# Dense expert products ahead of the lists, dense buffers in three pools, a third set of split halves, gelu two steps later, planner rate 430

## The chip, the core and the metric

The kernel runs on one core of a Trainium2 chip. The core has a matrix engine (TensorE, in the profile PE, its weight loads PEld), a vector engine (DVE), an activation engine (ACT), GpSimd (POOL), which issues the gathers here, and SyncE (SP), which issues the plain loads. The metric is the device time of one launch in microseconds, as the median over runs.

## What is computed

One residual layer over 1024 tokens of width 1024: three token mixers on a normalised input, gated and summed, and then an expert mixer (PEER). Only the second half matters here, cut to its core:

```python
q = (hf @ w_q).reshape(T, 8, 2, 128)
sc = jnp.einsum('thpd,hpkd->thpk', q, subkeys)
s1, i1 = lax.top_k(sc[:, :, 0], 16)
s2, i2 = lax.top_k(sc[:, :, 1], 16)
cand = (s1[..., :, None] + s2[..., None, :]).reshape(T, 8, 256)
top_s, pos = lax.top_k(cand, 16)
idx = jnp.take_along_axis(cand_idx, pos, axis=-1)   # of 16384 experts
gate = jax.nn.softmax(top_s, axis=-1)
act = jax.nn.gelu(jnp.einsum('chkd,cd->chk', u[ic], hc), approximate=False)
out = jnp.einsum('chk,chkd->cd', gate * act, v[ic])
```

Each token picks 16 of 16384 experts in each of 8 heads; each picked expert is a row of `u` and a row of `v`, of 4 KB each.

## The kernel before

**Tokens.** The 1024 tokens are 8 tiles of 128. The front (mixers, projections, norm, expert queries) runs in three groups of 2, 3 and 3 tiles (`GROUPS`, function `phase1`). After a group, `topk` (line 963) makes the lists of experts of its tiles in small steps that are kept in `side` and handed out one at a time by `sides` (line 1369).

**Two ways to the experts.** Six tiles gather: class `Experts` fetches by indirect DMA from POOL one row of `u` for each of 128 tokens (`fetch`, line 1082), DVE multiplies and sums it with the token (`step`, line 1122), a gelu of 32 such results follows on ACT, and 34 steps after the row of `u` the row of `v` is fetched; PE adds four rows of `v` at a time into two banks (`sum`, line 1155). That is 768 fetches of `u` and 768 of `v`. There are 5 buffers for rows of `u`, 8 for rows of `v`.

The tiles 4 and 6 (`DENSE`) are computed densely, over all 16384 experts: 128 blocks `e` of 128 experts, 256 tokens. For a block: a product with `u` and a gelu; a multiplication with the gate matrix; a product with `v` summed over all blocks in four banks. Two forms of the product with `u` exist. `early` takes plain f32 operands, for the first `RUN` = 22 blocks, and its results wait in `w`. `product` takes operands split into a high and a low half (`split`: ACT copies the high half, DVE subtracts to get the low one), three matmuls for each piece of the depth. The products with `v` (`weigh` and the loop behind it) use split halves of `v` and of `w`.

**Order in `dense` (line 1234).** It waits until the lists of both dense tiles are stored (`while len(stored) < ND`), with 1500 ns booked for each empty step. Then `wait[0]` stops the lists, the tokens are loaded, and `gate_matrix` (line 1192) builds the gate matrix for the last of the two tiles in 80 steps; every fifth step runs one `early`. The rest of the 22 follow, then the main loop: in step `e` the product of block `e + 22`, `weigh(e + 1)`, and the four banks' sums of block `e`. `take` makes the halves of `u` one block ahead; `weigh` makes those of `v` in the step before their use.

**Buffers.** `front.close()` gives back the front's memory (pools `const`, `wp`, `wide`, `big`, `act`, `kvp`, `tmp`, `small`, in this order of addresses); the dense part's one pool `dp` is laid over all of it. Scores from which the lists are made lie in `sc`, which is not part of the front, and for the middle tile of a group of three in `wide`, which is.

**The planner.** What is interleaved with what is fixed when the program is built. The loop at the end of `block_kernel` keeps two clocks in ns, `pe` and `dma`. A step of the gather (one row of `u`, one of `v`) adds 520 ns for the sum to `pe` and its bytes over `bw` to `dma`; a step of the front or of `dense` (`fill`) adds the estimate of its matmuls times `slow` and its loads over `bw`. `due` moves on at least 1500 ns for each kind of row in a step.

```python
least = LEAST * ((len(ex.todo) > 0) + (len(ex.vs) > 0))
due = max(due + least, pe - least)
while filler[0] is not None and (dma > pe or pe < due):
    a, b = fill(1)
```

`fill(1)` also hands out one step of the lists. `BW` is the rate in bytes per ns in the front (305) and after it (460). ACT and POOL run in program order; the order on the other engines is set by the scheduler of the language.

Of the kernel before, what the change touches and what calls it, by code (L numbers as in the profile page):

```python
# [7 lines left out]
F32 = mybir.dt.float32  # L8
# [26 lines left out]
RUN = 22  # L35


BW = 305.0, 460.0
SLOW = 1.38, 1.1
SUM_NS, ROW_BYTES = 520.0, 128 * 4096 + 12 * 1024.0  # L40
LEAST = 1500.0
# [38 lines left out]
def block_kernel(ctx: ExitStack, tc: tile.TileContext, io):  # L80
# [29 lines left out]
    def bank():  # L110
        return ps.tile([128, 512], F32, name="bank")
# [963 lines left out]
    class Experts:  # L1075
# [46 lines left out]
        def step(self):  # L1122

            self.run_behind()
            if not self.todo:
                return
            t, k = self.todo.pop(0)
            u = self.us.pop(0)
            nc.vector.scalar_tensor_tensor(u, u, 1.0, t["h"], op0=OP.mult, op1=OP.mult,  # L1129
                                           accum_out=t["parts"][:, k:k + 1])  # L1130
            b, c, j = k // 32, k % 32 // QB, k % QB
            self.behind.append([None] * (VLAG - 1) + [lambda: self.fetch("v", t["iT"][:, c, j, b:b + 1])]
                               + [None] * (SLAG - VLAG - 1) + [(lambda: self.sum(t, b, c, j)) if j % SUMS == SUMS - 1 else None])
            if k % 32 == 31:
                self.behind.append([lambda: self.gelu(t, b), lambda: self.scale(t, b), None,
                                    lambda: self.turn(t), lambda: self.weights(t, 0)])

        def gelu(self, t, b):
# [94 lines left out]

    def dense():
        st = ctx.enter_context(ExitStack())
        dp = st.enter_context(tc.tile_pool(name="dp", bufs=2))
        late_pool.append(dp)
        while len(stored) < ND:
            cost[0] += 1500
            yield  # L1240
        wait[0] = True
        whole = dp.tile([128, C, D], F32, name="vr")
        for i in range(ND):
            load(whole[:, i].rearrange("p (k t) -> p k t", k=KD), h2d[i])
        hh = dp.tile([128, KD, TD], F32R, name="hh", bufs=1)
        hl = dp.tile([128, KD, TD], F32R, name="hl", bufs=1)

        def split_tokens():
            for i in range(ND):
                r = whole[:, i].rearrange("p (k t) -> p k t", k=KD)  # L1250
                c = slice(i * 128, (i + 1) * 128)
                actf(hh[:, :, c], r, AF.Copy)
                nc.vector.tensor_sub(hl[:, :, c], r, hh[:, :, c])

        def raw(src, name):
            r = dp.tile([128, C, D], F32, name=name)
            load(r, src)
            return r

        def split(r, x, name):  # L1260
            hi = dp.tile([128, D], F32R, name=name + "h")
            lo = dp.tile([128, D], F32R, name=name + "l")
            actf(hi, r[:, x], AF.Copy)
            nc.vector.tensor_sub(lo, r[:, x], hi)  # L1264
            return hi, lo

        ur, us, ws, vr, gts = {}, {}, {}, {}, {}

        def near(e):
            if e % C == 0:  # L1270
# [1 line left out]
            return ur[e // C]  # L1272

        def take(e):
            us[e] = split(near(e), e % C, "u")

        def early(e):
            a = bank()[:, :TD].rearrange("p (i t) -> p i t", i=ND)
# [5 lines left out]
            actf(w.rearrange("p (i t) -> p i t", i=ND), a, AF.Gelu)  # L1284

        def product(e, a):
            if e + 1 < 128:
                take(e + 1)
            uh, ul = us.pop(e)
            for k in range(KD):  # L1290
                kc = slice(k * 128, (k + 1) * 128)
                mmr(a, uh[:, kc], hh[:, k, :], start=k == 0, stop=False, skip_group_check=True)
                mmr(a, ul[:, kc], hh[:, k, :], start=False, stop=False, skip_group_check=True)
                mmr(a, uh[:, kc], hl[:, k, :], start=False, stop=k == KD - 1, skip_group_check=True)
            w = ws[e] = dp.tile([128, TD], F32, name="w", bufs=RUN + 2)
            actf(w, a, AF.Gelu)
# [3 lines left out]
                gts[b] = dp.tile([128, TD // 32, 8, 32], F32, name="g")  # L1300
                load(gts[b], gd[:, :, 8 * b:8 * b + 8, :].rearrange("b p i t -> p b i t"))

        ur[0] = raw(io["uT"][0], "ur")
        e = steps = 0
        while next(gates) < ND:
            steps += 1
            cost[0] += 800
# [1 line left out]
                early(e)  # L1309
                e += 1  # L1310
            yield
        split_tokens()
        early(e)
        gate_load(0)
        vr[0] = raw(io["vd"][0], "vr")
        for e in range(e + 1, RUN):
            yield
            early(e)
        take(RUN)
        yield  # L1320
        behind[0], wait[0] = True, False

        sums = [[bank() for _ in range(2)] for _ in range(ND)]
        ab = bank().rearrange("p (x n) -> p x n", x=2)

        def weigh(e):
            if e % 8 == 0:
# [1 line left out]
            w = ws.pop(e)  # L1329
            nc.vector.tensor_mul(w.rearrange("p (b t) -> p b t", t=32), w.rearrange("p (b t) -> p b t", t=32),  # L1330
                                 gts[e // 8][:, :, e % 8, :])
            wh = dp.tile([128, TD], F32R, name="wh")
            wl = dp.tile([128, TD], F32R, name="wl")
            actf(wh, w, AF.Copy)
            nc.vector.tensor_sub(wl, w, wh)
            if e % C == 0:
                vr[e // C + 1] = raw(io["vd"][e // C + 1], "vr") if e + C < 128 else None
            return wh, wl, *split(vr[e // C], e % C, "v")

        now = weigh(0)  # L1340
        for e in range(128):
            if e + RUN < 128:
# [12 lines left out]
                yield  # L1355
            now = nxt
        for i in range(ND):
            r = dp.tile([128, C, D], F32, name="ur")[:, 0]
            load(r, xres[DENSE[i]])
            for half in range(2):  # L1360
                f = slice(half * 512, (half + 1) * 512)
# [123 lines left out]
```

## Time and profile before

| what | value |
|---|---|
| time, three runs | 3655.71, 3656.19, 3662.34 us; median 3656.19 |
| the profiled execution | 3664.29 us, its span 3662.5 us, mean granted clock 0.935 |
| moved by DMA | 1182.29 MB, mean 323 GB/s over the span |
| rows of u on DVE (768) | 933.3 us busy, mean 1220 ns; 605.8 us idle before them, 508.9 of it for the row to land |
| products with split u (3 x 848 matmuls) | 244.3 + 243.0 + 242.0 us |
| products with split v (3 x 512 matmuls) | 212.5 + 212.2 + 208.3 us |

Page, part 2: the span in 40 slices of 91.6 us; each digit of the first rows is a share in tenths, PEclk the clock granted to PE.

```profile
PE   7999979988999889899889898946867888889899
DVE  5443597555444568886655554889756766666645
PEclk9999989998999999999999999968888999999999
DMA  4435678989899997899887999879999999999995
GB/s 160 123 117 169 209 250 327 370 308 342 307 384 366 391 348 278 309 343 374 299 317 279 364 360 377 300 277 393 389 387 398 410 409 402 379 385 392 382 358 180
```

The front ends in slice 27 (2405 us), where PE falls to 4 and 6 tenths; the dense main loop starts at about 2716 us, in slice 30. A busy PE is not PE at its peak: ends of matmuls are modelled and they overlap.

### The profile page before, as it was taken

The page shows a single profiled execution, that of the slowest core. Times are in us where ns is not written, and L with a number is a line of the kernel's source. Part 1 is how long each engine was busy: PE and PEld are TensorE (multiplying, and loading weights), DVE is VectorE, ACT ScalarE, POOL GpSimd, SP SyncE. Part 2 cuts the span into 40 slices and gives each one's busy share as a digit, 9 for nine tenths or more (in the row PEclk, how much of TensorE's full clock was granted, in tenths as well). Part 3 has the DMA queues.
Part 4 walks back from the last instruction along what each step waited for, and adds up shares of the span by engine and source line. Part 5 has one row for each costly group of instructions (what it writes and reads, how often), then busy time and mean ns, then how long its engine had stood idle before and what let it go on. Part 6 is the DMA issues. An engine that isn't in the chain of part 4 may idle for free.

```text
span 3662.5 us, 59007 instructions
## 1 busy us (share of the span) xinstructions
PE 3182.7 (87%) x22418; PEld 2381.9 (65%) x22418; DVE 2295.9 (63%) x5873; ACT 994.8 (27%) x2065; POOL 1764.4 (48%) x1543
## 2 busy tenths in 40 slices
PE   7999979988999889899889898946867888889899
PEld 6889856655556666666555557734655767777677
DVE  5443597555444568886655554889756766666645
ACT  4442223332100123342322111111222333333334
POOL 0000046645565555566454555356656665655540
PEclk9999989998999999999999999968888999999999
DMA  4435678989899997899887999879999999999995
GB/s 160 123 117 169 209 250 327 370 308 342 307 384 366 391 348 278 309 343 374 299 317 279 364 360 377 300 277 393 389 387 398 410 409 402 379 385 392 382 358 180
DMA packets 343084, 1182.29 MB, mean 323 GB/s; under 512 B 38480, under 2 KB 79952, under 8 KB 323344
## 3 DMA queue, kind: packets, MB, share of 16 engines
q0 software_dynamic: 221184, 805.40, 58.2%
q1 hardware_dynamic: 100848, 336.37, 25.2%
q10 hardware_dynamic: 20768, 36.74, 2.6%
q8 instruction: 177, 2.90, 0.3%
q14 instruction: 107, 0.88, 0.1%
HBM read 1140.61 MB, written 37.75 MB: 322 GB/s over the span
## 4 chain that ended last, share of the span: by engine, by line
PE 46%; DMA 17%; DVE 13%; issue 13%; POOL 5%; ACT 2%; another core or an unknown queue 2%; ACTq 0%; SPq 0%; POOLq 0%; DVEq 0%
PE bank L118 31%; PE bank L1184 8%; DMA u<-in_u,iI 7%; DMA v<-in_v,iT 6%; DVE u L1129 3%; POOL v L1085 3%; PE poa L1163 3%; PE pob L1163 3%; POOL u L1085 2%; PE bank L122 1%; DMA ur<-in_uT 1%; DMA w<-in_w_gate 1%; ACT e L129 1%; DVE ab L1208 1%
## 5 line engine op out<-in xcount | busy, mean ns | idle before, releaser
L1085 POOL DMA_INDIRECT u<-in_u,iI x768 | 881.0, 1147 | 950.8 <-DVE wide L330 471.9
L1129 DVE SCALAR_TENSOR_TENSOR u<-u,h 128x1024 f32<-128x1024 f32 x768 | 933.3, 1220 | 605.8 <-DMA u<-in_u,iI 508.9
L1085 POOL DMA_INDIRECT v<-in_v,iT x768 | 882.7, 1149 | 853.1 <-PE pob L1163 349.5
L118 PE MATMUL bank<-wide,w 128*128 128x384 f32 x1536 | 523.3, 495 | 14.2 <-DVE wide L330 5.3
L118 PEld LDWEIGHTS bank<-wide,w 128*128 128x128 f32 x1536 | 292.3, 193 | 219.1 <-issue 21.3
L118 PE MATMUL bank<-w,wide 128*128 128x128 f32 x2304 | 277.2, 279 | 20.4 <-issue 17.5
L118 PEld LDWEIGHTS bank<-w,wide 128*128 128x128 f32 x2304 | 267.7, 194 | 35.4 <-issue 28.0
L1163 PE MATMUL pob<-v,wz 128*32 128x256 f32 x3072 | 231.8, 414 | 66.7 <-DMA v<-in_v,iT 61.0
L1184 PE MATMUL bank<-hh,uh 128*128 128x256 f32 x848 | 244.3, 288 | 30.4 <-ACT uh L129 19.0
L1184 PE MATMUL bank<-vl,wh 128*128 128x512 f32 x512 | 212.5, 415 | 51.4 <-DVE vl L1264 42.1
L118 PE MATMUL bank<-big,w 128*128 128x256 f32 (+1 forms) x1280 | 244.1, 347 | 10.7 <-issue 9.1
L1184 PE MATMUL bank<-hh,ul 128*128 128x256 f32 x848 | 243.0, 287 | 11.6 <-DVE ul L1264 10.6
L1163 PE MATMUL poa<-v,wz 128*32 128x256 f32 x3072 | 217.8, 405 | 29.1 <-DMA v<-in_v,iT 20.9
L1184 PE MATMUL bank<-hl,uh 128*128 128x256 f32 x848 | 242.0, 285 | 0.0
L118 PEld LDWEIGHTS bank<-big,w 128*128 128x128 f32 x1280 | 210.0, 196 | 43.7 <-issue 21.6
L129 ACT ACTIVATE e<-bank 128x512 f32<-128x512 f32 (+2 forms) x208 | 110.0, 529 | 448.2 <-PE bank L118 296.2
L1184 PE MATMUL bank<-vh,wh 128*128 128x512 f32 x512 | 212.2, 415 | 0.7 <-ACT vh L129 0.7
L1184 PE MATMUL bank<-vh,wl 128*128 128x512 f32 x512 | 208.3, 407 | 0.0
L1163 PEld LDWEIGHTS pob<-v,wz 128*32 128x32 f32 x3072 | 101.1, 117 | 162.3 <-issue 61.8
L129 ACT ACTIVATE w<-bank 128x256 f32<-128x256 f32 x128 | 49.1, 385 | 573.9 <-PE bank L1184 412.1
L1184 PEld LDWEIGHTS bank<-hh,uh 128*128 128x128 f32 x848 | 164.8, 194 | 40.5 <-ACT uh L129 19.1
L1163 PEld LDWEIGHTS poa<-v,wz 128*32 128x32 f32 x3072 | 98.4, 115 | 124.4 <-issue 47.6
(292 smaller groups left out, 5508.8 us busy)
## 6 DMA issues: line engine op xcount, KB each, us to landing
ur<-in_uT SPq DMA_DIRECT2D x64, 1024.0 KB
vr<-in_vd SPq DMA_DIRECT2D x64, 1024.0 KB
w<-in_w_in SPq DMA_DIRECT2D x102, 512.0 KB
w<-in_w_gate SPq DMA_DIRECT2D x72, 512.0 KB
w<-in_w_pq SPq DMA_DIRECT2D x48, 512.0 KB
g<-gd SPq DMA_DIRECT2D x16, 1024.0 KB
w<-in_w_o SPq DMA_DIRECT2D x48, 256.0 KB
w<-in_w_out SPq DMA_DIRECT2D x24, 512.0 KB
```

The costliest lines, as they stand in the source:

```text
L118: nc.tensor.matmul(out, lhsT, rhs, **kw)
L122: nc.tensor.transpose(out, in_, ident)
L129: nc.scalar.activation(out, in_, f, **kw)
L1085: nc.gpsimd.indirect_dma_start(out=t, out_offset=None, in_=io[kind], in_offset=bass.IndirectOffsetOnAxis(ap=ap, axis=0))
L1129: nc.vector.scalar_tensor_tensor(u, u, 1.0, t["h"], op0=OP.mult, op1=OP.mult, accum_out=t["parts"][:, k:k + 1])
L1163: nc.tensor.matmul(o[32 * k:32 * k + 32], t["wz", c][:, x, :], vs[y][:, 256 * k:256 * k + 256], start=b == 0 and x == SUMS - 1 and c % 2 == 0,
L1184: nc.tensor.matmul(out, lhsT, rhs, **kw)
L1208: nc.vector.tensor_scalar(ab[:, 0, x], iota, sl[:, 0, t + x:t + x + 1], sl[:, 2, t + x:t + x + 1], op0=OP.is_equal, op1=OP.mult)
```

## The change

- `BW` after the front is 430 in place of 460.
- The gelu of 32 gathered results, its scaling, its transposition and its first weights come two steps of the gather later.
- `dense` has three pools. `da` (raw tiles of `u`, high halves of `v`, halves of `w`, and a pad) covers `const` and `wp`; `db` (split tokens and high halves of `u`) has the size of `wide` and covers it; `dp` (raw tiles of `v` and the tokens, low halves, results, gates) covers the rest.
- The tokens and the first tiles of `u` are loaded as soon as the front is closed, and `early` products run while the lists are made, each with one more step of the lists.
- Halves of `u` are made two blocks ahead instead of one; halves of `v` one step earlier than before. Every third pair of halves lies in a buffer of `sc`, once the lists are all made. The halves of `w` have three buffers each in place of two.

```diff
-BW = 305.0, 460.0
+BW = 305.0, 430.0
...
             if k % 32 == 31:
-                self.behind.append([lambda: self.gelu(t, b), lambda: self.scale(t, b), None,
+                self.behind.append([None, None, lambda: self.gelu(t, b), lambda: self.scale(t, b), None,
                                     lambda: self.turn(t), lambda: self.weights(t, 0)])
...
     def dense():
         st = ctx.enter_context(ExitStack())
-        dp = st.enter_context(tc.tile_pool(name="dp", bufs=2))
+        da, db, dp = (st.enter_context(tc.tile_pool(name="d" + x, bufs=2)) for x in "abc")
         late_pool.append(dp)
-        while len(stored) < ND:
-            cost[0] += 1500
-            yield
-        wait[0] = True
+        first = da.tile([128, C, D], F32, name="ur")
+        da.tile([128, 64], F32, name="pad", bufs=1)
         whole = dp.tile([128, C, D], F32, name="vr")
+        load(first, io["uT"][0])
         for i in range(ND):
             load(whole[:, i].rearrange("p (k t) -> p k t", k=KD), h2d[i])
-        hh = dp.tile([128, KD, TD], F32R, name="hh", bufs=1)
-        hl = dp.tile([128, KD, TD], F32R, name="hl", bufs=1)

         def split_tokens():
+            hh = db.tile([128, KD, TD], F32R, name="hh", bufs=1)
+            hl = db.tile([128, KD, TD], F32R, name="hl", bufs=1)
...
+            return hh, hl

         def raw(src, name):
-            r = dp.tile([128, C, D], F32, name=name)
+            r = (da if name == "ur" else dp).tile([128, C, D], F32, name=name)
             load(r, src)
             return r

-        def split(r, x, name):
-            hi = dp.tile([128, D], F32R, name=name + "h")
-            lo = dp.tile([128, D], F32R, name=name + "l")
+        def split(r, x, name, n):
+            if n % 3 == 2 and not side:
+                both = sc.tile([128, 16, 128], F32, name="sc").rearrange("p a b -> p (a b)").bitcast(F32R)
+                hi, lo = both[:, :D], both[:, D:]
+            else:
+                hi = (da if name == "v" else db).tile([128, D], F32R, name=name + "h")
+                lo = dp.tile([128, D], F32R, name=name + "l")
             actf(hi, r[:, x], AF.Copy)
             nc.vector.tensor_sub(lo, r[:, x], hi)
             return hi, lo
...
         def take(e):
-            us[e] = split(near(e), e % C, "u")
+            us[e] = split(near(e), e % C, "u", e)
...
         def product(e, a):
-            if e + 1 < 128:
-                take(e + 1)
+            if e + 2 < 128:
+                take(e + 2)
...
-        ur[0] = raw(io["uT"][0], "ur")
         e = steps = 0
+        while len(stored) < ND:
+            if e < RUN:
+                early(e)
+                e += 1
+                sides(1)
+            else:
+                cost[0] += 1500
+            yield
+        wait[0] = True
         while next(gates) < ND:
...
-        split_tokens()
-        early(e)
+        hh, hl = split_tokens()
         gate_load(0)
         vr[0] = raw(io["vd"][0], "vr")
-        for e in range(e + 1, RUN):
+        for e in range(e, RUN):
+            early(e)
             yield
-            early(e)
         take(RUN)
+        take(RUN + 1)
         yield
...
+        vs = {}
+
+        def take_v(e):
+            if e % C == 0:
+                vr[e // C + 1] = raw(io["vd"][e // C + 1], "vr") if e + C < 128 else None
+            vs[e] = split(vr[e // C], e % C, "v", e)
+
         def weigh(e):
...
-            wh = dp.tile([128, TD], F32R, name="wh")
-            wl = dp.tile([128, TD], F32R, name="wl")
+            wh = da.tile([128, TD], F32R, name="wh", bufs=3)
+            wl = da.tile([128, TD], F32R, name="wl", bufs=3)
             actf(wh, w, AF.Copy)
             nc.vector.tensor_sub(wl, w, wh)
-            if e % C == 0:
-                vr[e // C + 1] = raw(io["vd"][e // C + 1], "vr") if e + C < 128 else None
-            return wh, wl, *split(vr[e // C], e % C, "v")
-
+            if e + 1 < 128:
+                take_v(e + 1)
+            return wh, wl, *vs.pop(e)
+
+        take_v(0)
         now = weigh(0)
...
         for i in range(ND):
-            r = dp.tile([128, C, D], F32, name="ur")[:, 0]
+            r = da.tile([128, C, D], F32, name="ur")[:, 0]
```

More of the change, by code (lines that the diff above doesn't have):

```diff
@@ L1265, in split @@
             return hi, lo
-        ur, us, ws, vr, gts = {}, {}, {}, {}, {}
+        ur, us, ws, vr, gts = {0: first}, {}, {}, {}, {}
         def near(e):
```

## The prediction

> **What bounds the kernel now.** I read the page first, for the busy shares, then the table of stages over the last third of the span, because the change touches nothing in the front but two steps of a 24-fold gelu. Columns of the table: stretch, its length, busy time (instructions) of PE, PEld, DVE, ACT and POOL, granted clock, DMA share, GB/s.
>
> ```profile
> PE 3182.7 (87%) x22418; PEld 2381.9 (65%) x22418; DVE 2295.9 (63%) x5873; ACT 994.8 (27%) x2065; POOL 1764.4 (48%) x1543
> q0 software_dynamic: 221184, 805.40, 58.2%
> ...
> 2405.00:2462.00 57.00, 15.71 (x144) 6.70 (x142) 46.84 (x217) 5.52 (x11) 33.34 (x31) 0.56 0.80 284
> 2462.00:2673.00 211.00, 150.50 (x1042) 113.60 (x1041) 170.90 (x548) 41.83 (x147) 145.52 (x119) 0.86 1.00 388
> 2673.00:2716.00 43.00, 20.92 (x128) 15.67 (x128) 13.97 (x28) 5.53 (x12) 17.04 (x16) 0.74 1.03 396
> 2716.00:3100.00 384.00, 325.90 (x2413) 262.98 (x2414) 261.03 (x409) 122.20 (x190) 240.66 (x189) 0.91 1.02 403
> 3100.00:3487.00 387.00, 337.62 (x2411) 273.26 (x2410) 248.35 (x382) 121.13 (x190) 216.45 (x176) 0.93 0.99 385
> 3487.00:3580.00 93.00, 86.70 (x737) 69.13 (x736) 40.39 (x57) 29.48 (x46) 39.52 (x37) 0.98 0.93 355
> 3580.00:3663.00 83.00, 77.99 (x397) 64.62 (x395) 45.01 (x57) 34.73 (x52) 0.00 (x0) 0.99 0.46 160
> ```
>
> PE's 87% is a mixture. From 2462 to 3487 the DMA engines are the full resource (share 0.99 to 1.03), whatever PE does. Two stretches leave them open: the 57 us in which the last lists are made (284 GB/s, PE busy 15.7 us), and the end, where POOL fetches nothing more and PE works through the rest of the dense chain alone. The chain of waits ends with that piece, and PE's order of time shows the hole before it:
>
> ```profile
> 3583.83 72.13 PE bank L1184 x339
> ...
> 2403.72 1.74 PE L118 MATMUL bank<-big,e 128*128 128x128 f32 x12
> 2416.68 3.64 PE L1163 MATMUL pob<-v,wz 128*32 128x256 f32 x32 [11.22 <-DMA v<-in_v,iT]
> ...
> 2461.65 0.42 PE L122 MATMUL bank<-ident,ab 128*128 128x128 f32 x1
> 2464.77 4.11 PE L118 MATMUL bank<-ab 128*128 128x128 f32 x16 [2.70 <-DVE ab L1208]
> ```
>
> The first row is the last 72 us: dense products with nothing beside them. The others are the front's last matmul, a row sum, the last transpose of the lists and the first gate.
>
> So the end is set by bytes, plus what the two open stretches waste. From 2462 on the table's rows add to 81.9 + 17.0 + 154.8 + 149.0 + 33.0 + 13.3 = 449 MB (length times GB/s). A fetch of one row per token is 805.40 MB / 1536 = 0.524 MB.
>
> **The change, part by part.**
>
> *Products during the lists.* `dense` needs 14 steps of the lists (7 for tile 5, 6 + 1 for tile 6). Before, each planner fill gave one; now each does one `early` product and gives two, so seven products run there.
>
> ```profile
> L118 PE MATMUL bank<-vr,ur 128*128 128x256 f32 x352 | 94.0, 421 | 10.8 <-ACT g L129 6.5 <-DMA ur<-in_uT 4.3
> ```
>
> One early product is 94.0/22 = 4.27 us, seven are 30 us, and PE has 41 us free in that hole, so they cost nothing; without that cover they cost their 30 us. What they move ahead is six loads on SP's queue (two halves of the tokens, five tiles of u): 6.3 MB into a stretch with 57 x (400 - 284) = 6.6 MB to spare (400 as in the full rows). SP then holds h's load for the next tile behind them; they wait only for the front's buffers, free at 2405, since the pool over `wide`, which the lists still read, holds only hh, hl and uh. The lists themselves are DVE's (46.8 of 57 us) and stay as long: I take 57 us; the three transposes and exps that may queue behind a product bound it at +13 us (three times 4.27), and 0 below.
>
> *Gates.* 80 steps are left, a product in every fifth: 15 of them, so none remain afterwards (six did: 26 us of PE in 2673 to 2716). The stage is full of bytes: 81.9 MB less a tile and the tokens (2.1) and four pairs of rows that the planner no longer puts there (4.2) is 75.6 MB, at 388 GB/s **195 us**. Splitting the tokens and loading the first gates and v stay: I take **20 us** of the 43 (bounds 10 and 43). The main loop starts at 2462 + 195 + 20 = **2677** instead of 2716. As the DMA was full meanwhile, this by itself gains only the 6.3 MB, 16 us.
>
> *Gelu two steps later.* 24 gelus; one alone waited long, with four gate copies behind it on ACT. Its wait hides under the gates' bytes: 0 taken, 19 us below.
>
> ```profile
> 2672.13 0.23 ACT L129 ACTIVATE gel<-parts 128x32 f32<-128x32 f32 x1 [18.80 <-DVE u L1129]
> ```
>
> *Third set, halves two ahead.* No instruction is added: 106 + 128 copies and as many subtractions as before. What it can remove is this (PE's waits, then DVE's, from 3100 to 3487, and one instance):
>
> ```profile
> PE bank L1184 <- DVE vl L1264: 36.1, 14, 5.4
> ...
> DVE u L1129 <- DMA u<-in_u,iI: 122.3, 40, 8.5
> ...
> 3286.76 1.23 DVE L1129 SCALAR_TENSOR_TENSOR u<-u,h 128x1024 f32<-128x1024 f32 x1 [1.43 <-DMA u<-in_u,iI]
> 3287.91 0.08 DVE L1129 DVE_READ_ACCUMULATOR u<-u,h 128x1 f32 x1
> 3287.91 1.22 DVE L1264 TENSOR_TENSOR vl<-vr,vh 128x1024 fp32r<-128x1024 f32 x1
> ...
> 3289.18 0.59 PE L1184 MATMUL bank<-vl,wh 128*128 128x512 f32 x1 [2.79 <-DVE vl L1264]
> ```
>
> DVE stands on a row that has not landed, vl stands behind it, PE stands on vl. With vl and ul a step earlier that wait goes. What is late next is wl, still made in the step before its use, behind the same row; it precedes vl by a subtraction (1.22 us), so short waits fall away and the longest (5.4) only shorten. Added waits: a copy that meets a busy buffer on ACT holds the gelu behind it, which PE needs 22 products later. I cost it at nothing.
>
> *Rate 430.* Per step of the dense loop the planner counts 1.1 x (2682 + 2696) ns = 5.92 us of PE, 1.18 MB of loads, and per pair of rows 1.073 MB against 0.52 us. At 460 a step takes (5.92 - 2.57)/(2.33 - 0.52) = 1.85 pairs, at 430 (5.92 - 2.74)/(2.50 - 0.52) = 1.61. The trace has 189 + 176 = 365 fetches to 94 copies of uh (47 + 47, below), 1.94 pairs, so the count is good to 5%.
>
> ```profile
> 2716.00:3100.00 384.00, 142.57 (x721) 119.31 (x721) 55.98 (x46) 48.38 (x47) 0.91 1.02 403
> 3100.00:3487.00 387.00, 143.67 (x752) 120.56 (x751) 57.18 (x47) 48.66 (x47) 0.93 0.99 385
> ```
>
> (the same table for uh alone; ACT's count is the copies). Carrying the counters through, before the rows end at step 97 of 128 and v's at 104, as in the trace; after, the dense loop ends with 9 rows of u and 43 of v to go: 52 fetches, 27.3 MB. So the end turns over: full DMA to the last, dense done first.
>
> *The tail of rows alone.* The nearest rows: 32 fetches of v with the dense chain beside them (first and last here, 68.7 us: 2.15 each), and back to back 0.94 + 0.30 = 1.24. The page's mean fetch is 1149 ns.
>
> ```profile
> 3499.29 0.94 POOL L1085 DMA_INDIRECT v<-in_v,iT  x1 [11.32 <-PE pob L1163]
> ...
> 3567.98 0.94 POOL L1085 DMA_INDIRECT v<-in_v,iT  x1 [0.30 <-issue]
> ...
> L1085 POOL DMA_INDIRECT v<-in_v,iT x768 | 882.7, 1149 | 853.1 <-PE pob L1163 349.5 <-PE poa L1163 263.4 <-issue 162.9
> ...
> 3484.83 0.40 PE L1184 MATMUL bank<-vh,wh 128*128 128x512 f32 x1
> ...
> 3487.57 0.28 PE L1184 MATMUL bank<-hh,uh 128*128 128x256 f32 x1
> ...
> 3490.45 0.39 PE L1184 MATMUL bank<-vh,wh 128*128 128x512 f32 x1
> ...
> 3498.35 1.93 PE L1163 MATMUL pob<-v,wz 128*32 128x256 f32 x32
> ```
>
> (The last four are PE's: the starts of a step's sums, of the next product, of the sums after it, and a warm row sum of four rows.)
>
> I take 1.15 + 0.30 and a little for buffers, 1.5: **78 us**; bounds 64 and 112. The last landing, sum, addition and store: 10 us. [...]
>
> *Sum.* Bytes of the main loop: 449 - 6.3 - 75.6 - 20 x 0.396 - 27.3 = 332 MB. The rate lay at 403 GB/s in the first half and at 385 in the second, where the vl waits stand; I take 398: 834 us (bounds 403: 824; 385: 862). End: 2677 + 834 + 78 + 10 = **3599**, 63 less than the span of 3662.5. That execution took 3664.3 and the median shown is 3656.2, so I take the 63 from the median: **3593**. A check by PE: sums 2.74 us (3484.83 to 3487.57), product 2.88 (to 3490.45), 1.61 rows at 1.93/4: 6.4 us of a step of (834 - 22 x 3.5)/106 = 7.1 us, 90%. From 3487 to 3580 PE was busy 93%, so that can be had.
>
> **Rivals.**
>
> 1. *The thinner ratio buys no pace* (slower). The main loop's steps take 387/47 = 8.2 us. If that comes from the ring DVE, row, PE, v buffer, POOL and not from bytes, fewer rows don't shorten it: 106 x 8.2 + 22 x 3.5 = 946, and rows still wait at the end: 2677 + 946 + 88 = 3711, **3705**. It decides above (3662.5 - 2677 - 88 - 77)/106 = 7.7 us a step. For it: PE lost 36.1 us to vl while DVE idled 122 us on rows. Against it: share 0.99 to 1.02, and the ring's waits are for landings, which thinner rows relieve. 0.13.
> 2. *wl takes vl's place.* Halves gain nothing, rate 385: 862, end 3627, **3621**. 0.17.
> 3. *The change doesn't do what it says*: the token or u buffers lie over something that the lists still hold, and the products start at 2462 after all. Then 6.3 MB (16 us) return: **3609**, with the tail as forecast. The old pool did load only at 2462, but there the code waited, too. 0.10.
> 4. *All of it works*: 403 GB/s, tail at 1.24: 3575, with the first stage of the loop at 10 us 3565, **3559**. 0.07.
>
> **How the numbers follow.** Forecast 3593 with 0.53 (3570 to 3618 by its own bounds). Faster by over 0.2% (what a measurement of this kernel can tell from no change, 7 us): 0.53 + 0.17 + 0.10 + 0.07 less 0.05 whose upper ends come within 7 us of 3656 when several bounds add up (lists +13, 862, tail 112): 0.82; same 0.05; slower 0.13. The range 3548 to 3650 leaves out the slower case and some of the rest.
>
> **What would show it.** Right: early products between 2405 and 2462, PE busy there over 40 us; DMA share near 1 until some 15 us before the end; POOL still fetching when the last dense matmul is done, some 52 fetches; uh copies every 7.1 us with 3.2 fetches each; PE's wait for vl gone from the steady stretch, granted clock there above 0.95. Wrong: vl's 36 us back under wl's name; steps of 7.7 us and more; a tail of rows above 110 us; lists that end after 2475 because a transpose stands behind a product that waits for its tile of u.

## The result, and the profile after

The changed kernel takes 3638.66 us (median of 20 runs, 3615.48 to 3656.92); the kernel before, run in between on the same chip, 3660.42 (20 runs, 3632.36 to 3682.16). The ratio is 0.9935, 95% interval 0.9916 to 0.9955: 0.65% faster, where 63 us or 1.7% were forecast. The profiled execution has a span of 3636.8 us (3662.5 before). Of all executions of the kernels below, three took far longer than the rest (16599.82 us in e12, 4892.24 and 5925.14 us in e17) and are in no ratio.

First the table of stages, in the stretches of the prediction (stretch, its length, busy time and instructions of PE, PEld, DVE, ACT, POOL, granted clock, DMA share, GB/s):

```profile
2405.00:2462.00 57.00, 34.41 (x242) 26.06 (x242) 45.25 (x211) 7.16 (x12) 28.95 (x27) 0.81 0.92 357
2462.00:2673.00 211.00, 144.19 (x985) 108.39 (x985) 171.18 (x537) 48.09 (x152) 126.95 (x116) 0.82 0.98 371
2673.00:2716.00 43.00, 32.22 (x220) 26.34 (x220) 27.75 (x48) 12.72 (x19) 21.41 (x17) 0.81 1.02 389
2716.00:3100.00 384.00, 342.26 (x2506) 283.77 (x2506) 256.89 (x401) 136.56 (x211) 205.51 (x164) 0.96 1.00 392
3100.00:3487.00 387.00, 346.14 (x2527) 286.54 (x2526) 253.05 (x386) 131.43 (x207) 206.63 (x168) 0.96 0.97 376
3487.00:3580.00 93.00, 80.22 (x494) 56.74 (x494) 62.53 (x100) 25.60 (x40) 54.63 (x47) 0.93 0.99 385
3580.00:3637.00 57.00, 27.99 (x288) 12.07 (x288) 2.78 (x7) 0.00 (x0) 27.39 (x30) 0.65 0.83 308
```

The hole of the lists is filled (357 GB/s in place of 284, PE 34 us in place of 16), and at the end rows are left over in place of dense work. But from 2716 to 3487 the DMA moves 392 and 376 GB/s, less than before (403 and 385), though PE has more done there and its clock is up from 0.91 and 0.93 to 0.96. Cut where this kernel's own stages lie, from the first to the last product with split `u`, then to the last dense matmul, then to the end:

```profile
2658.00:3479.00 821.00, 721.27 (x5251) 597.02 (x5251) 543.04 (x840) 279.24 (x432) 438.06 (x349) 0.95 0.99 384
3479.00:3565.00 86.00, 80.18 (x479) 58.03 (x477) 60.18 (x94) 28.48 (x44) 51.20 (x43) 0.98 0.98 383
3565.00:3637.00 72.00, 33.90 (x360) 14.60 (x360) 9.17 (x20) 0.23 (x1) 36.14 (x39) 0.66 0.87 329
```

The first row holds 106 steps of 821/106 = 7.75 us; 7.1 were forecast. Some 15 us of it are one wait in the first step, PE's for `wh` and DVE's for the gates, which land late:

```profile
2683.78 0.80 PE L1184 MATMUL bank<-vh,wh 128*128 128x512 f32 x1 [14.72 <-ACT wh L129]
...
2682.85 0.76 DVE L1349 TENSOR_TENSOR w<-w,g 128x256 f32<-128x256 f32 x2 [14.02 <-DMA g<-gd]
```

The same table, divided behind that wait:

```profile
2658.00:2684.00 26.00, 6.75 (x57) 4.41 (x57) 10.55 (x16) 2.34 (x4) 10.75 (x8) 0.65 1.02 397
2684.00:3479.00 795.00, 714.52 (x5195) 592.60 (x5196) 532.49 (x825) 276.91 (x429) 427.31 (x341) 0.96 0.98 384
```

So the steady step is 795/105 = 7.57 us. The loop of the kernel before:

```profile
2716.00:3595.00 879.00, 765.21 (x5675) 618.28 (x5676) 555.40 (x856) 277.15 (x432) 496.63 (x401) 0.93 0.99 386
```

Its steps took 8.29 us (there the first gates are waited for in front of the loop), with 401 fetches on POOL beside them in place of 349. What PE waited for most in that stretch before (who waited for whom, total, times, longest):

```profile
PE bank L1184 <- DVE vl L1264: 42.1, 16, 5.4
```

The same view of the changed kernel, from 2658 to 3479:

```profile
PE bank L1184 <- DVE wl L1354: 48.1, 29, 8.6
PE bank L1184 <- ACT wh L129: 20.9, 2, 14.7
```

The changed kernel's order of time around one of these waits, PE's rows and then DVE's (start, length, engine, line, operation, in brackets the idle time before and what ended it):

```profile
2846.33 0.39 PE L1184 MATMUL bank<-vl,wh 128*128 128x512 f32 x1
2850.50 0.79 PE L1184 MATMUL bank<-vh,wl 128*128 128x512 f32 x1 [3.78 <-DVE wl L1354]
...
2848.54 1.23 DVE L1129 SCALAR_TENSOR_TENSOR u<-u,h 128x1024 f32<-128x1024 f32 x1 [5.83 <-DMA u<-in_u,iI]
2849.69 0.08 DVE L1129 DVE_READ_ACCUMULATOR u<-u,h 128x1 f32 x1
2849.69 0.42 DVE L1349 TENSOR_TENSOR w<-w,g 128x256 f32<-128x256 f32 x1
2850.03 0.42 DVE L1354 TENSOR_TENSOR wl<-w,wh 128x256 fp32r<-128x256 f32 x1
```

It is the picture of before with another name: DVE stands 5.83 us on a row that has not landed, `w` and `wl` stand behind it, PE stands on `wl`. The wait for `vl` (42.1 us in the loop before) is gone, and 48.1 us of `wl` have come. All of PE's idle time together is 114 us of 879 before, 1.07 us a step, and 80 of 795 now (behind the first step), 0.77 a step.

### The profile page after: what moved, and what is told of

It reads as the page before. It is cut to its first block, busy times and chain, and to the rows that moved or that the text cites. A ratio compares the mean times of both kernels' runs of the same rounds, so it can differ in the third digit from the quotient of the medians.

```text
span 3636.8 us, 59087 instructions
## 1 busy us (share of the span) xinstructions
PE 3172.6 (87%) x22418; PEld 2380.4 (65%) x22418; DVE 2288.9 (63%) x5873; ACT 995.2 (27%) x2063; POOL 1761.0 (48%) x1543
## 4 chain that ended last, share of the span: by engine, by line
PE 42%; DMA 19%; issue 15%; DVE 14%; POOL 5%; another core or an unknown queue 2%; ACT 2%; ACTq 0%; SPq 0%; POOLq 0%; DVEq 0%
PE bank L118 29%; DMA u<-in_u,iI 9%; PE bank L1184 7%; DMA v<-in_v,iT 5%; DVE u L1129 4%; POOL u L1085 3%; PE poa L1163 2%; POOL v L1085 2%; PE pob L1163 2%; DMA vr<-in_vd 1%; DMA gd<-g 1%; PE bank L122 1%; DMA g<-gd 1%; ACT e L129 1%
## 5 line engine op out<-in xcount | busy, mean ns | idle before, releaser
L1085 POOL DMA_INDIRECT v<-in_v,iT x768 | 876.4, 1141 | 890.8 <-PE poa L1163 350.9
L118 PE MATMUL bank<-w,wide 128*128 128x128 f32 x2304 | 286.4, 284 | 22.5 <-issue 16.2
L118 PEld LDWEIGHTS bank<-w,wide 128*128 128x128 f32 x2304 | 276.5, 199 | 37.6 <-issue 27.4
L1163 PE MATMUL poa<-v,wz 128*32 128x256 f32 x3072 | 205.0, 400 | 19.0 <-DMA v<-in_v,iT 17.0
L1184 PE MATMUL bank<-vh,wl 128*128 128x512 f32 x360 | 149.6, 417 | 45.4 <-DVE wl L1354 41.1
L1184 PE MATMUL bank<-hh,uh 128*128 128x256 f32 x600 | 174.0, 290 | 13.0 <-ACT w L129 9.2
L1184 PE MATMUL bank<-hl,uh 128*128 128x256 f32 x600 | 172.6, 288 | 0.6 <-issue 0.6
L1184 PE MATMUL bank<-hh,ul 128*128 128x256 f32 x600 | 172.8, 288 | 0.4 <-issue 0.4
L1184 PE MATMUL bank<-vh,wh 128*128 128x512 f32 x360 | 150.2, 417 | 15.9 <-ACT wh L129 15.9
L118 PE MATMUL bank<-oT,w 128*128 128x384 f32 (+1 forms) x480 | 152.0, 455 | 0.0
L1184 PE MATMUL bank<-vl,wh 128*128 128x512 f32 x360 | 146.8, 408 | 2.9 <-DVE vl L1268 1.8
```

What stands on the lines that cost most here:

```text
L118: nc.tensor.matmul(out, lhsT, rhs, **kw)
L1085: nc.gpsimd.indirect_dma_start(out=t, out_offset=None, in_=io[kind], in_offset=bass.IndirectOffsetOnAxis(ap=ap, axis=0))
L1163: nc.tensor.matmul(o[32 * k:32 * k + 32], t["wz", c][:, x, :], vs[y][:, 256 * k:256 * k + 256], start=b == 0 and x == SUMS - 1 and c % 2 == 0,
L1184: nc.tensor.matmul(out, lhsT, rhs, **kw)
```

## The experiments

Each ratio is against runs of the kernel before made in between on the same chip. Chips differ: those medians lay between 3552.55 and 3678.21 us, and the front alone took 2303 to 2436, so stages are counted from the front's end. The table is from the traces; "low half" is what PE waited for `wl`, or `vl`, in the product loop, "sums" what POOL waited there for PE's sums of `v` to free a buffer, and "tail" the time behind the last dense matmul.

| kernel | us a step | GB/s in the loop | low half, us | sums, us | tail, us | front's end to end | ratio [95%] |
|---|---|---|---|---|---|---|---|
| before (460) | 8.29 | 386 | vl 42 | 189 | 4 | 1257 | 1 |
| after (430) | 7.75 | 384 | wl 48 | 246 | 72 | 1234 | 0.9935 [0.9916, 0.9955] |
| e1 w ahead, 430 | 7.49 | 395 | w 31 | 181 | 74 | 1222 | 0.9901 [0.9867, 0.9936] |
| e2 after, 460 | 8.26 | 398 | wl 37 | 138 | 5 | 1235 | 0.9939 [0.9915, 0.9964] |
| e3 before, 430 | 7.99 | 366 | vl 88 | 324 | 38 | 1289 | 1.0071 [1.0042, 1.0100] |
| e4 old halves, 430 | 8.21 | 365 | vl 82 | 334 | 71 | 1304 | 1.0122 [1.0075, 1.0168] |
| e5 w ahead, 445 | 7.80 | 400 | w 28 | 125 | 9 | 1190 | 0.9858 [0.9831, 0.9885] |
| e6 old halves, 460 | 8.53 | 388 | vl 65 | 192 | 4 | 1235 | 0.9981 [0.9964, 0.9999] |
| e7 before, new halves, 460 | 8.14 | 395 | wl 47 | 147 | 4 | 1234 | 0.9952 [0.9934, 0.9970] |
| e8 gelu back | 7.69 | 387 | wl 55 | 247 | 74 | 1219 | 0.9930 [0.9903, 0.9957] |
| e9 after again | 7.72 | 386 | wl 64 | 242 | 74 | 1229 | 0.9963 [0.9946, 0.9980] |
| e10 after, 445 | 7.97 | 394 | wl 58 | 160 | 8 | 1206 | 0.9904 [0.9880, 0.9928] |
| e11 w ahead, 430 again | 7.55 | 393 | w 32 | 180 | 73 | 1218 | 0.9934 [0.9911, 0.9957] |
| e12 w ahead, 445 again | 7.79 | 401 | w 29 | 122 | 10 | 1180 | 0.9846 [0.9826, 0.9866] |
| e13 buffers 6 and 7 | 7.62 | 389 | wl 47 | 260 | 81 | 1236 | 0.9969 [0.9938, 0.9999] |
| e14 buffers 4 and 9 | 7.83 | 384 | wl 62 | 231 | 72 | 1240 | 0.9967 [0.9936, 0.9999] |
| e15 sums of two | 7.43 | 384 | wl 48 | 265 | 66 | 1232 | 0.9849 [0.9792, 0.9906] |
| e16 w ahead, 445, sums of two | 7.57 | 400 | vl 26 | 168 | 5 | 1199 | 0.9733 [0.9674, 0.9792] |
| e17 before, sums of two | 8.11 | 389 | vl 44 | 149 | 5 | 1253 | 0.9910 [0.9870, 0.9951] |
| e18 after, third time | 7.74 | 385 | wl 49 | 242 | 73 | 1241 | 0.9930 [0.9901, 0.9959] |

("w 31" is PE's wait for ACT's `w`, the gelu of a product; there `wl` no longer appears. "us a step" is the loop over its 106 steps; the kernels with products during the lists have the wait for the first gates in it, up to 0.16 us a step.)

### Does `wl` hold the loop up, and what are the halves worth?

Theory: the pace at 430 is set by PE and by what PE waits for; a half made earlier takes its wait away, until the next is late. Rival: the waits only show that the DMA is full, and nothing is won by moving them.

e1 makes the halves of `w` one block earlier, as the change does with those of `v`:

```diff
-        def weigh(e):
+        hw = {}
+
+        def take_w(e):
...
+            hw[e] = wh, wl
+
+        def weigh(e):
             if e + 1 < 128:
+                take_w(e + 1)
                 take_v(e + 1)
-            return wh, wl, *vs.pop(e)
-
+            return *hw.pop(e), *vs.pop(e)
+
+        take_w(0)
         take_v(0)
```

> The changed kernel, but the halves of w for block e+2 are made while block e is summed, as those of v already are (buffers are there: three each). Theory A (wl took vl's place: it is still made in the step before its use, behind the same unlanded row on DVE, and holds PE): PE's 48.1 us on wl from 2720 to 3480 fall below 15, the main loop's step falls from 7.5 us towards 7.1, ratio to before 0.981 to 0.989 instead of 0.9935. Theory B (at this mix the DMA engines give some 385 GB/s and no more, the waits only show it): wl's wait turns into another one on a row or a buffer, step 7.5 us, ratio 0.990 to 0.996. Theory C (the gather's ring: v fetches on POOL wait for sums that stand behind dense matmuls in PE's order, 246 us of 760): half of A's gain at most, POOL's wait for the sums stays above 200 us.

e4 undoes the new halves and keeps the rest (the main lines of its edit follow); e7 puts the new halves alone on the kernel before, at its 460:

```diff
-            if n % 3 == 2 and not side:
+            if False:
...
-            if e + 2 < 128:
-                take(e + 2)
+            if e + 1 < 128:
+                take(e + 1)
...
-            if e + 1 < 128:
-                take_v(e + 1)
+            take_v(e)
```

> The changed kernel with the split halves as before: u one block ahead, v in the step before its use, two sets, nothing in sc. What is left is the products during the lists, the pools, the gelu and the rate. If the third set is worth what the prediction said (vl's waits of 36 us in 387 gone, then replaced by wl's): with theory A 5 to 15 us slower than the changed kernel (ratio 0.995 to 0.999), PE's wait for vl back at 60 us or more over the main loop. With theory B no difference: ratio 0.992 to 0.996.

> The kernel before with the split halves alone as in the change: two blocks ahead, every third pair in sc, v a step earlier; rate 460, nothing runs during the lists, old gelu. A (full of bytes at 460): DMA rate in the main loop from 394 to at most 400 GB/s, ratio 0.994 to 1.000, the last 60 to 75 us of dense alone stay. If the halves carry the whole gain of the change: ratio 0.985 to 0.992.

The row of stages for e1's loop, and what its PE waited for most in it:

```profile
2689.00:3483.00 794.00, 712.45 (x5252) 598.68 (x5252) 540.96 (x836) 282.26 (x433) 452.09 (x350) 0.95 1.00 395
```

```profile
PE bank L1184 <- ACT w L129: 31.1, 13, 6.9
```

The same of e4:

```profile
2680.00:3550.00 870.00, 745.34 (x5292) 615.44 (x5293) 549.25 (x847) 277.07 (x432) 407.51 (x353) 0.92 0.95 365
```

```profile
PE bank L1184 <- DVE vl L1268: 82.3, 29, 5.7
```

At 430 the loop goes from 8.21 (old halves) to 7.75 (the change) to 7.49 (halves of `w` ahead, too) with the same rows beside it (353, 349 and 350 fetches), and the DMA rate follows: 365, 384, 395. So at 430 the bytes did not bound the first two; PE's waits did, and each half that is moved gives pace. The new halves are worth 1.6 to 1.9% there (1.0122 to the change's 0.9963 to 0.9930 in three measurements). At 460 they are worth 0.4 to 0.5% (e6 0.9981 to e2 0.9939; e7 0.9952).

The time follows e1's pace less surely: 0.9901 against 0.9935, and when it was run beside the changed kernel on another chip (e11 and e9) 0.9934 against 0.9963. Each pair's intervals overlap; taken alone, neither shows a gain. e1 met none of its three theories whole: the wait moved on, to `w`, and the time is in B's range, but a limit of some 385 GB/s, B's reason, is out. e4 lost more than either theory had (0.999 at most), with `vl`'s wait back as A had it; e9 lies just above what was expected of it.

> The changed kernel unaltered, so that the other three have it beside them. Expected 0.9935 of before (0.991 to 0.9955), product loop 7.7 us a step, a tail of rows alone of 70 to 75 us.

> The changed kernel with the halves of w one block earlier, rate 430. First measured at 0.9901 of before, with an interval that overlaps that of the changed kernel. If the halves of w ahead are worth something by themselves, it is 0.3% or more below the changed kernel beside it (7.5 us a step against 7.75 over 106 steps are 27 us less, 10 of which may return in the rest). If not, both are the same within 0.2%.

### What is the rate worth?

Edits of one line (`BW = 305.0, 460.0` on the changed kernel and on e4, `BW = 305.0, 430.0` on the kernel before).

> The changed kernel with the planner's rate back at 460. If the ratio turned the end over as the counters say: the dense chain ends last again with some 14 blocks alone (40 us at less than half the DMA rate), rows of u end near block 103, and the time is 10 to 20 us above the changed kernel (ratio to before 0.996 to 1.000). If the thinner ratio costs as much pace in the main loop (DMA rate 394 before, 384 after) as it gains at the end: within 6 us of the changed kernel, ratio 0.992 to 0.996, main loop back at 390 GB/s or more.

> The kernel before with the planner's rate alone at 430. Counters: rows end at block 125 of 128 and 27 fetches of v are left, so dense and rows end nearly together and the last 72 us of dense alone go. If the end alone counts: 25 to 40 us faster, ratio 0.989 to 0.993. If the thinner ratio slows the loop (vl's waits unchanged, pace 8.2 us kept with fewer rows): no gain or slower, ratio 0.998 to 1.012.

> The changed kernel with split halves as before and the rate at 460: what is left is the products during the lists, the pools and the later gelu. It is the fourth cell beside the changed kernel (0.9935), e2 (0.9939) and e4 (1.0122). If the halves matter only where rows are thin, because at 460 the loop is full of bytes anyway (A): close to e2, ratio 0.993 to 0.999, step 8.2 to 8.4 us. If the halves are worth as much at 460 as at 430 (1.9%): ratio 1.010 to 1.016. If the products during the lists themselves pay the 16 us that the prediction gave them, the ratio is below 0.998.

With the old halves 430 loses: e3 is 0.7% slower than before, e4 1.4% slower than e6. Rows come thinner, but PE waits twice as long for `vl` (88 us for 42) and the DMA falls to 366 GB/s; that is the first rival of the prediction. Why `vl` is later with thinner rows, no run shows. With the new halves 430 and 460 give the same, 0.9935 and 0.9939. The loop of e2 and its rest, to set beside the three rows of the changed kernel:

```profile
2698.00:3574.00 876.00, 752.19 (x5592) 613.78 (x5596) 576.91 (x895) 279.88 (x435) 521.68 (x410) 0.93 1.01 398
3574.00:3667.00 93.00, 83.42 (x500) 58.70 (x496) 37.90 (x54) 28.91 (x44) 20.11 (x20) 0.94 0.65 235
```

460 leaves 93 us at 235 GB/s, which costs 93 x (1 - 235/398) = 38 us; 430 leaves a tail of 72 us at 329, 12 us by the same sum, but runs 907 us at 384 in place of 398, 32 us. So what thin rows won at the end, 26 us, they gave back in the loop.

Between them both ends meet. e5 and e12 take 445 with the halves of `w` ahead, e10 takes 445 alone:

> The changed kernel with the halves of w a step earlier (as in e1) and the planner's rate at 445. By the counters u's rows end at block 114 and v's at 127 of 128, so neither rows nor dense blocks stand alone at the end; e1 had 38 fetches of v alone after the last dense matmul, 74 us. Theory A (end and pace are two terms): the tail falls from 74 us to under 25, the loop's step goes from 7.5 to 7.8 us, 10 to 20 us faster than e1, ratio to before 0.984 to 0.989. Theory B (from the front's end on only bytes count, some 390 GB/s, and ratio and end give back to each other what they take, as e2 against the changed kernel): as e1, ratio 0.988 to 0.993.

> The changed kernel with rate 445 in place of 430, nothing else. If the unbalanced end is the loss (a tail of 72 us with 300 GB/s), 445 ends rows and dense blocks together and gains most of what halves of w ahead with 445 gained, 0.988 or better. If the waits for the low halves in the loop are the loss, the wl wait stays (about 45 us in 760) and the ratio stays at 0.992 to 0.995, like 430 and 460.

> Halves of w one block earlier and rate 445, a second time: 0.986 expected. If the two parts add, its distance to the changed kernel is the sum of the other two distances; if 445 only pays with the halves of w ahead, it is more than the sum.

```profile
2549.00:3375.00 826.00, 731.80 (x5392) 609.95 (x5395) 559.41 (x870) 281.12 (x434) 495.68 (x382) 0.94 1.01 401
3375.00:3478.00 103.00, 92.42 (x668) 64.32 (x664) 50.98 (x77) 29.00 (x44) 52.39 (x50) 0.97 0.98 383
3478.00:3488.00 10.00, 2.00 (x33) 0.94 (x32) 1.22 (x3) 0.00 (x0) 0.00 (x0) 0.91 0.45 165
```

These are e12's loop, rest and end: 401 GB/s, and rows and dense blocks end within 10 us of each other. The same of e10:

```profile
2567.00:3411.00 844.00, 733.99 (x5387) 603.21 (x5387) 560.28 (x874) 279.31 (x432) 490.04 (x382) 0.94 1.00 394
3411.00:3518.00 107.00, 95.12 (x672) 63.89 (x670) 48.88 (x75) 28.92 (x45) 49.92 (x49) 0.97 0.94 356
3518.00:3526.00 8.00, 1.93 (x32) 0.94 (x32) 0.70 (x2) 0.00 (x0) 0.00 (x0) 0.90 0.45 159
```

On one chip stand 0.9963 (the change), 0.9934 (halves of `w`), 0.9904 (445) and 0.9846 (both): the two parts add up to 0.88%, together they measured 1.17%, more than the sum by less than the intervals. 445 alone keeps `wl`'s wait (58 us) and still gains 0.6%, between the two answers expected. That gain is not the balanced end: from the loop's start each of these kernels moves 372 MB, and by the sum above (against 398 GB/s) e10 loses 8 us in the loop and 16 behind it, the changed kernel 29 and 16. 445 has nearly the loop's rate of 460 and, behind the loop, the loss of 430 and not the 38 us of 460.

### The gelu two steps later

e8 puts the gelu back to its place, and the two products' steps stay:

> The changed kernel with the gelu and what follows it at the old step. The prediction took it as hidden. If so: ratio to before 0.991 to 0.996, as the changed kernel. If a gelu that waits on ACT for its last row holds the copies behind it (18.8 us once, before): 5 to 15 us slower, ratio 0.996 to 0.999, and ACT's wait of gel for DVE u comes back in the trace.

0.9930 against 0.9935, and 7.69 us a step against 7.75: no difference, as costed.

### Is it the ring of the buffers of `v`?

Over the kernels so far the DMA rate falls as POOL waits longer for the sums of `v` (122 us: 401 GB/s; 334 us: 365). Either that ring (row, PE's sum, buffer, POOL) causes the lower rate, or the wait only shows how far POOL is ahead. Three edits change the ring: 6 and 7 buffers for `u` and `v` in place of 5 and 8, 4 and 9 (so the buffers of `u` go the other way), and sums of two rows, which free buffers in pairs (`SUMS = 2`, with the gelu at its old place, since the weights must be there sooner).

> The changed kernel with 6 buffers for rows of u and 7 for rows of v in place of 5 and 8. In the product loops measured so far the DMA rate falls as POOL's wait for the sums of v grows (122 us: 401 GB/s, 246 us: 384, 334 us: 365). If that ring (row, PE's sum, v buffer, POOL) sets the rate, one v buffer less makes the wait longer and the loop slower: POOL's wait above 280 us, rate under 380 GB/s, 8.0 us a step or more, ratio 0.998 or above. If POOL's wait is only a sign that the DMA is full, the time stays within 0.3% of the changed kernel (0.9935 to 0.9963).

> The changed kernel with 4 buffers for rows of u and 9 for rows of v. If the ring of v sets the rate and u has buffers to spare, POOL's wait for sums falls under 220 us and the rate rises to 388 GB/s or more, ratio 0.991 or below. If the buffers of u matter as much (DVE waits for rows of u 180 us in the same stretch), it is slower than the changed kernel. If neither matters, within 0.3% of it.

> The changed kernel with the gelu at its old place (measured as no difference) and PE adding two rows of v at a time in place of four, as often as before in all. A pair of buffers comes free after two rows, no buffer is added. If the ring of v sets the rate: POOL's wait for sums under 180 us, 390 GB/s or more, product loop 7.5 us a step, ratio 0.990 or below. If not: 0.992 to 0.997.

e13's loop in the table of stages, and POOL's waits in it:

```profile
2678.00:3486.00 808.00, 721.84 (x5261) 595.85 (x5265) 540.82 (x836) 279.51 (x435) 434.13 (x350) 0.95 0.99 389
```

```profile
POOL v L1085 <- PE poa L1163: 145.4, 20, 17.7
POOL v L1085 <- PE pob L1163: 115.0, 22, 15.0
```

The same of e15:

```profile
2647.00:3435.00 788.00, 730.52 (x5192) 591.81 (x5196) 530.91 (x807) 279.77 (x432) 427.75 (x338) 0.96 0.99 384
```

```profile
POOL v L1085 <- PE poa L1163: 138.1, 34, 12.2
POOL v L1085 <- PE pob L1163: 126.8, 30, 13.0
```

None of the three does what the ring as the cause asks for: one buffer of `v` less leaves 389 GB/s and 7.62 us (under 380 and 8.0 were expected), one more 384 and 7.83, and sums of two neither shorten POOL's wait (265 us) nor raise the rate; e15's step of 7.43 us has fewer fetches beside it (338) and hardly a wait for the first gates (1.62 us). That speaks for POOL's wait as a sign. More it does not show, since the first two edits moved that wait by 15 us only and changed the buffers of `u` with it.

Yet e15 is faster, 0.9849, and with `w` ahead and 445 the best of all:

> Halves of w one block earlier, rate 445, gelu at its old place, sums of two rows. Without the sums of two it measured 0.9846 to 0.9858, with 401 GB/s in the product loop and POOL's wait at 122 us. If the ring still costs there, 0.983 or below; if 401 GB/s is as much as the DMA gives, no difference, 0.984 to 0.987.

Its trace says that the gain is not behind the front: from the front's end to the end it takes 1232 us, as the changed kernel does. The front was shorter, 2353 us beside 2422 and 2385 of e13 and e14. So sums of two went onto the kernel before, with the changed kernel on the same chip:

> The kernel before with sums of two rows in place of four, nothing else. With the change's other parts they measured 0.9849, but their trace has 1232 us from the front's end to the end, as the changed kernel has (1234), and a shorter front. If sums of two gain in the front, this kernel gains there too: 0.985 to 0.991, the front 30 us or more shorter than that of the changed kernel beside it, 1250 to 1265 us behind it. If they gain only together with early products and halves ahead, 0.995 to 1.005.

> The changed kernel once more, beside the one above, so that the two fronts come from one chip: 0.9935 to 0.9965, the front as long as that of the kernel before (its code is the same but for the gelu's place).

The first 2300 us of e17, then of e18:

```profile
0.00:2300.00 2300.00, 2116.18 (x14717) 1510.33 (x14721) 1410.37 (x3878) 625.09 (x1391) 1049.23 (x954) 0.96 0.83 305
```

```profile
0.00:2300.00 2300.00, 2072.15 (x14408) 1499.45 (x14409) 1371.06 (x3694) 616.54 (x1363) 1028.04 (x932) 0.95 0.81 298
```

In the same time e17's PE does 309 matmuls more; its front ends at 2362 us, e18's at 2408; the 1253 us behind it are those of the kernel before (1257). The gain of sums of two (0.991, about 33 us) is the front's, where in these traces 63% of all rows are fetched (504 + 466 of 1536 in e18); the dense part has none of it. The 46 us between the two fronts are one pair of executions, and e18's, 3652.18 us, is the longest of its seven, so the ratio is the safer measure. Why the front likes them was not tried.

e16 is the version that beats both kernels by most: 3562.06 us beside 3659.22, 0.9733.

## Why the forecast was too low

Its sign was right, its size was not. Of the signs of being wrong that it named, two are there: `vl`'s wait under `wl`'s name, and steps of 7.7 us and more (7.75 over the loop). By its own steps, the forecast first and the measurement behind the colon, all from the profiled execution (sum 3599, measured 3636.8):

**Lists, 57 us: 65 (59 before, by the same cut from the front's last matmul to the first gate).** Seven products ran there, as forecast, with PE at 34 us (over 40 was named) and the lists some 6 us longer, inside the bound of 13. PE's order of time shows the first part of it, a wait for the tokens, whose load goes out only when the front is closed:

```profile
2412.37 2.05 PE L118 MATMUL bank<-vr,ur 128*128 128x256 f32 x4 [9.62 <-DMA vr<-h2d]
...
2425.68 13.76 PE L118 MATMUL bank<-vr,ur 128*128 128x256 f32 x60
...
2443.02 10.63 PE L118 MATMUL bank<-vr,ur 128*128 128x256 f32 x48
```

Bytes moved ahead: 57 x (357 - 284) = 4.2 MB; 6.3 were forecast. The third rival (the products start at 2462 after all) is out. What early bytes are worth can be seen in e6: products during the lists, pools and gelu of the change without its halves and its rate are 0.9981, 7 us, of 16.

**Gates, 195 + 20 us: 185 + 5.** The main loop starts at 2658, 19 us ahead of the forecast 2677. But the loading of the first gates, which the 20 us held, was only pushed into the loop's first step: PE runs steadily from 2684, 7 us after 2677. The DMA moves 397 GB/s meanwhile, so no bytes are lost by it.

**Halves, "what is late next is wl ... short waits fall away and the longest only shorten": this step failed.** 29 waits of 48 us in place of 16 of 42. The order of the queue was read rightly; that `wl` precedes `vl` by one subtraction was taken for a gain, but all that DVE makes in a step stands behind the same row, so its first piece is as late as its last to within 1.2 us, and the waits are up to 8.6. At the same rate of 430 the new halves do shorten the waits (e4: 29 of 82.3 us together); but the step was worked out from the waits at 460, and thinner rows double them (42 to 88 us on the kernel before, e3). The second rival is the case that came true, by its mechanism and by its rate, 385 GB/s (384 measured); it gave 3621.

**The main loop, 332 MB at 398 GB/s, 834 us: the term that carries the error.** It measured 821 + 86 = 907 us, with 821 x 0.384 + 86 x 0.383 = 348 MB. Of the 73 us more, 348/0.398 - 834 = 40 are 16 MB that earlier starts and a shorter tail had moved into it, and they are made good there (19 us before the loop, 16 behind it). The other 33 are the rate. 38 us is all that the sum missed.

The rate was taken from the kernel before, whose loop was nearly full of bytes (the new halves alone raise its 386 GB/s to 395, e7), for one with an eighth fewer rows to the step (349 fetches to 106 steps, 401 before). Here a steady step has 795 x 0.384/105 = 2.91 MB, 7.3 us at 398 GB/s, and 714.5/105 = 6.8 us of busy PE; it took 7.57, more than either, since PE stood. The check by PE was short as well: it had 6.4 us of busy PE to a step, from one instance. That the DMA share lay at 0.99 to 1.02 was brought against the first rival, and that reading was wrong: the share is 0.99 at 384 GB/s here, 0.95 at 365 in e4, 1.01 at 401 in e12. So it does not show how much more the engines could move.

**The first rival (slower, 3705) needed 7.7 us a step to decide**, and 7.75 were measured over the loop, 7.57 behind its first step. It did not come out slower, since the steady step is below 7.7 and less was left behind the loop than that sum had. On the old halves it is what happens (e3, e4), and what was said against it, that its waits are for landings which thinner rows relieve, failed there.

**Tail, 52 fetches at 1.5 us, 78, and 10 for the end: 72 in all.** The price was right, the count was not. (The upper bound of 2.15 us a fetch came from a wrong count: from 3499.29 to 3567.98 the kernel before has 36 fetches, not 32, 1.96 us each.) POOL's order of time:

```profile
3565.68 0.94 POOL L1085 DMA_INDIRECT v<-in_v,iT  x1 [0.31 <-issue]
3566.92 0.94 POOL L1085 DMA_INDIRECT v<-in_v,iT  x1 [0.30 <-issue]
...
3576.76 0.93 POOL L1085 DMA_INDIRECT v<-in_v,iT  x1 [2.69 <-PE pob L1163]
...
3622.31 0.94 POOL L1085 DMA_INDIRECT v<-in_v,iT  x1 [1.28 <-remote]
```

38 fetches start from 3565.68 to 3622.31, 56.63/37 = 1.53 us each: 0.94 + 0.30 in a run, 46 us in all, and now and then a wait, some 11 us, about half of it for sums. The last landing, sum, addition and store took 14.5 us. So the tail was not 1.24 us a fetch, as the fourth rival had it. A single fetch took 0.93 to 1.02 us there, with DVE busy for 9 of the 72 us, where the page of the profile has 1141 ns in the mean; why it is shorter there, no run shows. The tail was longer by those waits. The granted clock is 0.66 there (0.98 in the stretch before it). The first sum, 0.87 us after the last dense matmul, took 1.93 us; the next eight took 2.37 to 3.64 us, each after a wait of 1.89 to 3.50 us, and this one 3.60. What lowers the clock, no run shows:

```profile
3604.38 3.60 PE L1163 MATMUL poa<-v,wz 128*32 128x256 f32 x32 [2.82 <-DMA v<-in_v,iT]
```

**Gelu, nothing: nothing** (e8). **From span to median** the forecast took off 6 us (3599 to 3593), since the profiled execution of before was that much above its median; that of after was 1.9 below its own. That is the other 8 us of the 46 by which 3593 was missed.

Still open: what the DMA could give at most in this mixture (no run had more than 401 GB/s over a loop), and what keeps e1's loop at 7.49 us with 6.7 of busy PE: at 395 GB/s it is within 1% of the 398 that the sum took, so it may be bytes again, or PE's many short waits.

## What to carry to other kernels

A rate measured where bytes are (nearly) the bound may not be carried to a mixture with fewer bytes: work out the step of each resource, add what the engines wait for one another, and treat a busy share near 1 as no proof that the resource is full (0.99 at 384 GB/s, 1.01 at 401). Where DVE stood on a landing (5.83 us in the instance shown), `w` and `wl` behind it were late with it; moving one product ahead handed PE's wait to the next (`vl` 42 us, then `wl` 48, then `w` 31), so move all of them. An interleaving fixed when the program is built is best tried at more than one rate: of the three here the middle one (445), where both kinds of work end together, was the fastest with the halves of `w` as they were and, against 430, with them ahead.

## What was not expected of the hardware

The length of the front differs by chip: 2309 to 2315 us in the traces of four kernels on one chip (e5 to e8), 2419 to 2436 in those of four on another (e1 to e4), with the same code there but for the gelu's place. The medians of the kernel before differ as much between these chips (3552.55 and 3678.21 us), while its runs on one of them lie within some 30 us. And adding rows in pairs, 16 matmuls at a time in place of 32, shortens the kernel before by about 33 us (e17), by the traces in its front, with the same number of matmuls.
